# ScalarE issues the stores of gates and activations in a PEER layer, and the dense part's loads of both

## The chip, the cores and the metric

The kernel runs on one core of a Trainium2 chip. The metric is the device time of one execution, in microseconds (us). The names of the engines are those of the profile: PE (TensorE, matmuls), PEld (its weight loads), DVE (VectorE), ACT (ScalarE), POOL (GpSimd), SP (SyncE). Every engine works off its own instructions in order. A DMA is issued by one engine's queue as one of its instructions, and moves its bytes without that engine.

## What is computed

One layer of an encoder for 512 prompt tokens (four tiles of 128) and 128 tokens of eight sample streams (one more tile). The part at issue is the feed-forward half, PEER: each token picks, by a query and two sets of 128 sub-keys, 16 experts in each of 8 heads, out of 128 x 128 experts.

```
y = h + peer(rmsnorm(h))                      # h: 2048 wide
peer: q = x @ w_query; scores per head against two sets of 128 sub-keys
      the 16 best of 128 x 128 sums per head -> expert ids, softmax gates
      a = gelu(x . U[id]);  out = sum over heads and picks of  gate * a * V[id]
```

After the layer comes a last norm. Arithmetic is f32.

## The kernel before

**Matmuls.** `gemm` (L193) streams a weight matrix in blocks `raw` of two k-rows (128x2x512 f32, 512 KB, L198, a ring of four buffers, issued by SP). `split` (L141) makes of each 128x512 half a rounded copy `whi` on ACT (L143) and the rest `wlo` on DVE (L144), in rings of five (six in the last part); PE does three 128x512 matmuls for each token tile (L211, L212, L213). After each block `pump()` advances the first generator in the list `side`, in which work that goes beside the gemms is cut into steps by `yield`; `tick()` advances the list `bg`, the PEER of two token tiles by gathered rows (POOL issues the gathers, DVE does L740 and L745). The order of each engine's instructions is fixed when the program is built: a scheduler places them by the order of the program text, these rates, priorities and cost estimates of its own.

**The PEER of the other three token tiles is dense.** Three pieces matter here:

- `weights` (L775): for each of the three tiles the gates are written out as a dense matrix of 128 tokens by 16384 experts, in 32 groups of four tokens, 96 in all. A group makes one-hot vectors on DVE (L789, L795) and, for two of the four tokens, on ACT (L792, L793); four f32 matmuls on PE (L796); a copy out of PSUM on ACT (L798, tile `s`); and a store of 256 KB to DRAM (L799, tensor `wd`).
- `U(s)` (inside `dense_peer`, L802): a gemm with 512 columns of U for three tiles; ACT takes the gelu (L829, tile `S`). For s under LEAD = 12 the result is stored to DRAM (L831, tensor `ad`), because the gates don't exist yet. These twelve gemms run beside the weights stage, which is in `side`.
- `h_step(s, i, a)` (L809): loads the tile's 512 gates from `wd` (L812, through `load`, L97, whose DMA is L99), multiplies with the activation (L814, DVE), transposes the product in four 128x128 pieces (L818, PE) and splits it into HT (L820, by L143 and L144; the tiles `m`), the stationary side of the V gemms. `late(s)` (L836) does this for the stored activations of the three tiles, and loads each of them first. `late(0)` and `late(1)` come into `side` at s = 8, behind what is left of the weights.

**The switch.** After U(11), `drain()` runs what is left in `side`, one set of pools is closed and another opened (L866 to L868), with 12 `s` buffers, D_STAGE `S` buffers, D_LOAD `b` buffers, 4 `raw`, 6 `whi` and `wlo`. Then come the gemms `V(b, nb)` (L841), b = 0 to 15, with the late h_steps of b + 1 and the U gemms from 12 on between them. For b = 0 the evict of V loads the residual `x1d` (L845) and adds it (L847).

All DMAs named here are issued by SP before the change, so gates, activations, residual and weight blocks stand in one queue, in the scheduler's order.

## Time and profile before

| | |
|---|---|
| median of 3 runs | 3991.54 us (3985.18 to 3993.43) |
| the profiled execution | 3996.57 us, its span 3994.9 us |
| PE, PEld | 97%, 80% of the span |
| DVE, ACT, POOL | 79%, 43%, 21% |
| DMA | 1180.51 MB, 296 GB/s on the mean |
| granted TensorE clock, mean | 0.99 |

Stages, from the trace: the G2 tiles' query ends at about 1660 us; routing goes to 1805; the weights stage runs from 1805 to 2160, beside the U gemms; the last UT matmul before the switch starts at 2205.59, the first V matmul at 2212.34; the dense gemms then go on to the end. "Busy" counts an instruction's whole duration; matmuls overlap, so that one of some 395 ns is followed by the next after some 227 ns. Idle time of PE is what can be won or lost; on another engine it matters only where PE ends up waiting for it.

### The profile page before, as it was taken

How to read it: one execution, taken by the hardware profiler on the slowest of the kernel's cores; microseconds unless marked ns; L12 is line 12 of the kernel's file. 1: busy time of each engine (PE TensorE's matmuls, PEld its weight loads, DVE VectorE, ACT ScalarE, POOL GpSimd, SP SyncE). 2: the span in 40 equal slices, each digit the busy share in tenths (PEclk: the TensorE clock that was granted, in tenths of full speed). 3: DMA queues.
4: the chain of work that ended last, by engine and by line, in shares of the span. 5: the costliest groups of instructions: out<-in, count | busy, mean ns of one | idle time of the engine just before them, and what ended most of it. 6: DMA issues, size and time to landing. Idle time of an engine off the chain costs nothing. (4 is left out here: it accounts for less than half of the span.)

```text
span 3994.9 us, 52665 instructions
## 1 busy us (share of the span) xinstructions
PE 3883.8 (97%) x17880; PEld 3177.5 (80%) x17880; DVE 3153.5 (79%) x5421; ACT 1728.2 (43%) x3338; POOL 829.1 (21%) x678
## 2 busy tenths in 40 slices
PE   8999998999999999999999899999999999999998
PEld 6778786877777888877878788877888888888886
DVE  4655769966767987899977688878888888888888
ACT  5665554444444334436665333333333333333333
POOL 1000113211212223211111112222222222222222
PEclk9999999999999999999999999999999999999999
DMA  7666786777878997569988989989998999999987
GB/s 224 204 187 208 248 264 201 273 276 279 311 277 286 336 334 249 206 198 314 327 264 288 338 325 338 342 299 365 338 350 336 353 331 345 345 340 349 346 337 290
DMA packets 333919, 1180.51 MB, mean 296 GB/s; under 512 B 35840, under 2 KB 94784, under 8 KB 267088
## 3 DMA queue, kind: packets, MB, share of 16 engines
q1 hardware_dynamic: 259824, 640.15, 47.9%
q0 software_dynamic: 73824, 536.99, 35.0%
q8 instruction: 141, 2.31, 0.2%
q14 instruction: 130, 1.06, 0.1%
HBM read 1117.69 MB, written 59.31 MB: 295 GB/s over the span
## 5 line engine op out<-in xcount | busy, mean ns | idle before, releaser
L211 PE MATMUL acc<-whi,m 128*128 128x512 f32 (+1 forms) x5232 | 2066.7, 395 | 23.3 <-ACT whi L143 18.3
L212 PE MATMUL acc<-wlo,m 128*128 128x512 f32 (+1 forms) x5232 | 2049.8, 392 | 22.5 <-DVE wlo L144 22.4
L213 PE MATMUL acc<-whi,m 128*128 128x512 f32 (+1 forms) x5232 | 2044.1, 391 | 0.3 <-DVE m L144 0.2
L143 ACT CAST whi<-raw 128x512 fp32r<-128x512 f32 (+1 forms) x1888 | 1157.9, 617 | 1979.3 <-PE acc L213 1646.6
L144 DVE TENSOR_TENSOR wlo<-raw,whi 128x512 fp32r<-128x512 f32 (+1 forms) x1824 | 1221.5, 689 | 526.8 <-ACT whi L143 523.1
L212 PEld LDWEIGHTS acc<-wlo,m 128*128 128x128 f32 x5232 | 990.7, 189 | 227.1 <-DVE wlo L144 34.5
L211 PEld LDWEIGHTS acc<-whi,m 128*128 128x128 f32 x5232 | 989.3, 189 | 225.4 <-ACT whi L143 20.6
L213 PEld LDWEIGHTS acc<-whi,m 128*128 128x128 f32 x5232 | 989.5, 189 | 202.7 <-DVE m L144 0.8
L740 DVE SCALAR_TENSOR_TENSOR gb<-gb,xa 128x2048 f32<-128x2048 f32 x256 | 589.6, 2303 | 79.5 <-DMA gb<-in_U,idx 69.1
L745 DVE SCALAR_TENSOR_TENSOR xa<-gb,hw,xa 128x2048 f32<-128x2048 f32 x239 | 560.3, 2344 | 70.4 <-DMA gb<-in_V,idx 64.1
L754 POOL DMA_INDIRECT gb<-in_V,idx x239 | 318.5, 1333 | 1228.8 <-DVE wlo L144 331.2
L754 POOL DMA_INDIRECT gb<-in_U,idx x256 | 339.6, 1327 | 1018.9 <-ACT whi L143 366.2
L144 POOL TENSOR_TENSOR wlo<-raw,whi 128x512 fp32r<-128x512 f32 x64 | 91.5, 1431 | 261.8 <-ACT whi L143 229.7
L796 PEld LDWEIGHTS pm<-s 128*128 128x128 f32 x768 | 102.6, 193 | 30.5 <-ACT s L793 14.6
L796 PE MATMUL pm<-s 128*128 128x128 f32 x768 | 113.7, 283 | 10.0 <-DVE s L789 8.0
L789 DVE TENSOR_SCALAR s<-io,S 128x128 f32<-128x128 f32 x384 | 114.8, 339 | 3.6 <-DMA wd<-s 3.6
L847 DVE TENSOR_TENSOR s<-s,acc 128x512 f32<-128x512 f32 x180 | 112.5, 678 | 0.0
L144 DVE TENSOR_TENSOR m<-pm,m 128x512 fp32r<-128x512 f32 (+1 forms) x142 | 93.5, 661 | 7.5 <-ACT m L143 6.5
L143 ACT CAST m<-pm 128x512 fp32r<-128x512 f32 (+1 forms) x142 | 79.6, 563 | 16.3 <-PE pm L362 6.3
L798 ACT COPY s<-pm 128x512 f32<-128x512 f32 x96 | 56.5, 588 | 64.8 <-PE pm L796 64.2
L814 DVE TENSOR_TENSOR b<-b,b 128x512 f32<-128x512 f32 x36 | 24.8, 688 | 56.0 <-DMA b<-wd 53.5
L792 ACT ACTIVATE s<-io,S 128x128 f32<-128x128 f32 x192 | 66.7, 398 | 3.6 <-DVE S L782 2.3
(194 smaller groups left out, 1668.7 us busy)
## 6 DMA issues: line engine op xcount, KB each, us to landing
raw<-in_UT SPq DMA_DIRECT2D x256, 512.0 KB, 6.2
raw<-in_VP SPq DMA_DIRECT2D x256, 512.0 KB, 6.5
raw<-in_w_in SPq DMA_DIRECT2D x224, 512.0 KB, 4.6
raw<-in_w_out SPq DMA_DIRECT2D x64, 512.0 KB, 5.4
raw<-in_w_q SPq DMA_DIRECT2D x64, 512.0 KB, 4.5
wd<-s SPq DMA_DIRECT2D x96, 256.0 KB, 6.0
b<-wd SPq DMA_DIRECT2D x96, 256.0 KB, 5.2
raw<-in_w_pa SPq DMA_DIRECT2D x32, 512.0 KB, 4.2
```

Of the source, the lines that this page charges most:

```text
L143: mark[0] = nc.scalar.copy(hi, src).ins
L144: (E or nc.vector).tensor_sub(lo, src, hi.bitcast(F32))
L211: nc.tensor.matmul(o, xh, hi, start=(k == 0), stop=False)
L212: nc.tensor.matmul(o, xh, lo, start=False, stop=False)
L213: nc.tensor.matmul(o, xl, hi, start=False, stop=(k == K - 1))
L740: q = nc.vector.scalar_tensor_tensor(t, t, 1.0, xg, op0=ALU.mult, op1=ALU.mult, accum_out=dots[:, j:j + 1])
L745: q = nc.vector.scalar_tensor_tensor(y, t, hw[:, j:j + 1], y, op0=ALU.mult, op1=ALU.add)
L754: d = nc.gpsimd.indirect_dma_start(out=t, out_offset=None, in_=src, in_offset=bass.IndirectOffsetOnAxis(ap=idx[j // 32][:, j % 32:j % 32 + ...
L789: nc.vector.tensor_scalar(a, io128, tr[:, 0, t:t + 1], tr[:, 2, t:t + 1], op0=ALU.is_equal, op1=ALU.mult)
L792: nc.scalar.activation(b, io128, AF.Abs, bias=tr[:, 3, t:t + 1])
L796: nc.tensor.matmul(pw[:, t - t0, :], a, b, start=True, stop=True)
L847: nc.vector.tensor_add(y[i, nb], x1, ps)
```

## The change

The stores of gates (L799) and activations (L831) and the loads of both in the dense part are issued by ACT's queue and no longer by SP's: 96 + 36 stores and 96 + 36 loads, 264 DMAs. Weight blocks and everything else stay with SP. `load` takes a tag, and after the switch the loads of activations have a ring "h" of their own with three buffers (D_ACT); D_LOAD goes from 4 to 3 and D_STAGE from 5 to 3. `h_step` is cut differently: loads, a `yield`, the mul, a `yield`, then the transposes. `late(s)` starts the loads of tile i + 1 next to the mul of tile i. For b = 0, V loads the residual straight into the `y` slots ahead of its gemm (SP), and the add is in place. Lines move by one from L98 on and by up to 15 further down.

```diff
-D_STAGE = 5
-D_LOAD = 4
+D_STAGE = 3
+D_LOAD = 3
+D_ACT = 3
...
-        def load(src, shape=(128, 512)):
-            t = pools["wk"].tile(list(shape), F32, name=nm("b"), tag="b", bufs=cfg["b"])
-            nc.sync.dma_start(t, src)
+        def load(src, shape=(128, 512), tag="b", E=None):
+            t = pools["wk"].tile(list(shape), F32, name=nm(tag), tag=tag, bufs=cfg["b"] if tag == "b" else D_ACT)
+            (E or nc.sync).dma_start(t, src)
             return t
...
                 nc.scalar.copy(w, pw)
-                nc.sync.dma_start(wd[ti][t0:t0 + 4, :].rearrange("t (i j) -> i t j", i=128), w)
+                nc.scalar.dma_start(wd[ti][t0:t0 + 4, :].rearrange("t (i j) -> i t j", i=128), w)
...
                 def h_step(s, i, a):
                     b, hf = divmod(s, 2)
+                    if a is None:
+                        a = load(ad[s][i], tag="h" if opened[0] else "b", E=nc.scalar)
+                    w = load(wd[G[i]][:, s * 512:s * 512 + 512], E=nc.scalar)
+                    yield
+                    nc.vector.tensor_mul(w, w, a)
+                    yield
                     if (b, i) not in HT:
                         HT[b, i] = mtile([128, 2, 8, 128], F32R)
-                    w = load(wd[G[i]][:, s * 512:s * 512 + 512])
-                    nc.vector.tensor_mul(w, w, a)
-                    yield
...
-                            nc.sync.dma_start(ad[s][i], a)
+                            nc.scalar.dma_start(ad[s][i], a)
...
                 def late(s):
+                    gens = [h_step(s, i, None) for i in range(n)]
+                    next(gens[0])
                     for i in range(n):
-                        a = load(ad[s][i])
-                        yield from h_step(s, i, a)
+                        next(gens[i])
+                        if i + 1 < n:
+                            next(gens[i + 1])
+                        yield
+                        for _ in gens[i]:
+                            yield
...
                 def V(b, nb, ticks):
                     def ev(i, ps):
-                        x1 = y.get((i, nb))
-                        if b == 0:
-                            x1 = load(x1d[i][:, nb * 512:nb * 512 + 512])
-                            y[i, nb] = slot()
-                        nc.vector.tensor_add(y[i, nb], x1, ps)
+                        nc.vector.tensor_add(y[i, nb], y[i, nb], ps)
...
+                    if b == 0:
+                        for i in range(n):
+                            y[i, nb] = slot()
+                            nc.sync.dma_start(y[i, nb], x1d[i][:, nb * 512:nb * 512 + 512])
```

The scheduler then orders the engines anew. Up to about 1715 us all of them keep their order. Three places change.

PE, the end of the last UT gemm, U(11). Before, the last of the six late transposes (four L818, `pm_20605`) stand here, with 54 matmuls of that gemm still behind them and, further down, the V gemms:

```order
9005 L212 MATMUL acc_20419<-wlo_20593,m_12743 128x512
9006 L213 MATMUL acc_20419<-whi_20592,m_12744 128x512
9007 L818 MATMUL pm_20605<-ident,b_20571 128x128 [waits PE_49]
9008 L818 MATMUL pm_20605<-ident,b_20571 128x128 x3
9009 L211 MATMUL acc_20417<-whi_20614,m_12739 128x512 [waits Activation_49]
9010 L212 MATMUL acc_20417<-wlo_20615,m_12739 128x512 [waits DVE_49]
9011 L213 MATMUL acc_20417<-whi_20614,m_12740 128x512
9012 L211 MATMUL acc_20418<-whi_20614,m_12741 128x512
9013 L212 MATMUL acc_20418<-wlo_20615,m_12741 128x512
9014 L213 MATMUL acc_20418<-whi_20614,m_12742 128x512
```

After, these are the last rows ahead of the first V matmul (`acc_20725`), and the last UT matmul is row 9032:

```order
9042 L822 MATMUL pm_20448<-ident,b_20365 128x128 [waits DVE_49,Activation_49]
9043 L822 MATMUL pm_20448<-ident,b_20365 128x128 x3
9044 L822 MATMUL pm_20495<-ident,b_20457 128x128 [waits DVE_49,PE_49]
9045 L822 MATMUL pm_20495<-ident,b_20457 128x128 x3
9046 L822 MATMUL pm_20535<-ident,b_20462 128x128 [waits DVE_49,PE_49]
9047 L822 MATMUL pm_20535<-ident,b_20462 128x128 x3
9048 L822 MATMUL pm_20605<-ident,b_20533 128x128 [waits DVE_49,PE_49]
9049 L822 MATMUL pm_20605<-ident,b_20533 128x128 x3
9050 L822 MATMUL pm_20797<-ident,b_20758 128x128 [waits DVE_49,PE_49]
9051 L212 MATMUL acc_20725<-whi_20730,m_20323 128x512 [waits Activation_49]
```

All six groups of late transposes, the first one of the next h_step (`b_20758`, of b = 1), and the last seven matmuls of the weights stage now stand between the last UT matmul and the first V matmul. Before, the last weights matmul stood 198 matmuls ahead of the end of U(11). In the stage itself, the 384 L796 rows stood in 132 places between UT matmuls and now stand in 195, over 1260 UT matmuls where there were 1062.

ACT, one group of the weights stage (`s_19685` is its pair of one-hots, `s_19653` the copy of the group before it). Before:

```order
1964 L798 COPY s_19653<-pm_19636 128x512 [waits DMAHW3_49,PE_49]
1965 L792 ACTIVATE s_19685<-io_82,S_19051 128x128 [waits DVE_49]
1966 L792 ACTIVATE s_19685<-io_82,S_19051 128x128
1967 L793 ACTIVATE s_19685<-s_19685 128x128 [waits Activation_49] x2
1968 L143 CAST whi_19793<-raw_19778 128x512 [waits PE_49]
1969 L143 CAST whi_19848<-raw_19846 128x512 [waits DMAHW4_49,DVE_49,PE_49]
```

After:

```order
2188 L799 COPY s_19653<-pm_19636 128x512 [waits PE_49]
2189 L793 ACTIVATE s_19685<-io_82,S_19051 128x128 [waits DMAHW1_49]
2190 L800 DMA wd_19046<-s_19653 128x4x128 [waits Activation_49]
2191 L794 ACTIVATE s_19685<-s_19685 128x128 [waits Activation_49]
2192 L793 ACTIVATE s_19685<-io_82,S_19051 128x128
2193 L144 CAST whi_20385<-raw_20370 128x512 [waits DVE_49,PE_49]
2194 L794 ACTIVATE s_19685<-s_19685 128x128 [waits Activation_49]
2195 L799 COPY s_19701<-pm_19684 128x512 [waits PE_49]
```

The store is now a row of ACT's, between the one-hot rows of the next group, and the wait for a free buffer (DMAHW) has gone from the copy to a one-hot row. Of the 96 store rows 45 wait for a DMA.

ACT at the switch, where SP had the loads before (rows 9 below):

```order
2315 L800 DMA wd_19046<-s_20283 128x4x128 [waits Activation_49]
2316 L144 CAST m_20398<-pm_20399 128x512 [waits PE_49]
2317 L100 DMA b_20365<-wd_19046 128x512 [waits DMAHW5_49,DMAHW4_49,DMAHW7_49,DMAHW3_49,DMAHW2_49]
2318 L100 DMA b_20455<-ad_15234 128x512
2319 L100 DMA b_20457<-wd_16498 128x512
2320 L100 DMA b_20460<-ad_15235 128x512 [waits DMAHW6_49,DVE_49]
2321 L144 CAST m_20447<-pm_20448 128x512 [waits PE_49]
2322 L100 DMA b_20462<-wd_17766 128x512
2323 L100 DMA b_20531<-ad_15236 128x512 [waits DMAHW4_49,DMAHW0_49,DVE_49]
2324 L144 CAST m_20323<-pm_20495 128x512 [waits PE_49]
2325 L100 DMA b_20533<-wd_19046 128x512 [waits DMAHW1_49]
2326 L144 CAST m_20398<-pm_20535 128x512 [waits PE_49]
```

Row 2317 is the first load of gates of the third tile (`wd_19046`). It waits for five DMA semaphores, those of that tile's stores, the last of which is row 2315; the loads behind it wait in ACT's order, some also for muls (DVE) or for casts standing ahead of them. Rows 2328 and 2329 are the loads of `h_20756` and `b_20758`, whose product is transposed in PE's row 9050, and row 2334 is the first `whi` of the V gemms.

## Rows read from the trace of the kernel before

**Rows 1.** The page, its first part: busy time, share of the span and instructions of each engine.
```profile
PE 3883.8 (97%) x17880; PEld 3177.5 (80%) x17880; DVE 3153.5 (79%) x5421; ACT 1728.2 (43%) x3338; POOL 829.1 (21%) x678
```

**Rows 2.** Busy time of each engine in stretches of the program (us of the stretch, its length, then busy time and number of instructions of each engine, the granted TensorE clock, the DMA engines' share and GB/s). In order: the weights stage, the switch, the first V gemms, and the bulk of the dense stage.
```profile
1810.00:2160.00 350.00, 340.04 (x1831) 284.47 (x1831) 305.20 (x730) 230.24 (x613) 50.10 (x41) 0.99 0.92 303
2160.00:2215.00 55.00, 48.63 (x221) 39.51 (x220) 35.28 (x38) 19.12 (x32) 9.55 (x8) 0.96 0.83 292
2215.00:2300.00 85.00, 80.39 (x357) 65.98 (x356) 63.54 (x75) 27.47 (x47) 15.30 (x11) 0.97 0.93 346
...
2750.00:3750.00 1000.00, 998.15 (x4482) 824.93 (x4481) 847.40 (x971) 346.94 (x568) 265.40 (x196) 1.00 0.92 344
```

**Rows 3.** What TensorE waited for between 1805 and 2310 us (engine, tile and line, what released it: us in total, times, longest).
```profile
PE pm L796 <- DVE s L789: 8.0, 1, 8.0
PE acc L211 <- ACT whi L143: 6.4, 1, 6.4
...
PE pm L818 <- DVE b L814: 4.6, 2, 3.3
PE pm L796 <- ACT s L793: 1.0, 1, 1.0
```

**Rows 4.** The timeline of SyncE's queue around the longest wait of rows 3 (start, us, what was issued).
```profile
2043.18 0.33 SPq L99 DMA_DIRECT2D b<-wd  x1
```

**Rows 5.** The timeline of VectorE in the same stretch (in brackets the idle time before, and what ended it).
```profile
2049.20 0.69 DVE L814 TENSOR_TENSOR b<-b,b 128x512 f32<-128x512 f32 x1 [8.68 <-DMA b<-wd]
```

**Rows 6.** Two short stretches with the columns of rows 2: right after that wait, and right after the switch.
```profile
2050.00:2060.00 10.00, 9.11 (x37) 7.84 (x38) 8.30 (x22) 4.28 (x12) 0.00 (x0) 0.67 0.43 115
...
2212.00:2220.00 8.00, 7.66 (x23) 5.87 (x24) 7.68 (x10) 4.23 (x8) 4.11 (x2) 0.68 1.04 417
```

**Rows 7.** The timeline of TensorE at the switch: the last matmul of the last UT gemm and the first three of the first V gemm.
```profile
2205.59 0.39 PE L213 MATMUL acc<-whi,m 128*128 128x512 f32 x1
2212.34 0.80 PE L211 MATMUL acc<-whi,m 128*128 128x512 f32 x1 [6.37 <-ACT whi L143]
...
2213.66 0.63 PE L213 MATMUL acc<-whi,m 128*128 128x512 f32 x1
2214.09 0.63 PE L211 MATMUL acc<-whi,m 128*128 128x512 f32 x1
```

**Rows 8.** The timeline of ScalarE at the switch.
```profile
2204.66 2.05 ACT L829 ACTIVATE S<-acc,stats 128x512 f32<-128x512 f32 x3 [8.22 <-PE acc L213]
2211.67 1.14 ACT L143 CAST whi<-raw 128x512 fp32r<-128x512 f32 x2 [4.97 <-DMA raw<-in_VP]
```

**Rows 9.** The timeline of SyncE's queue at the switch.
```profile
2205.38 1.68 SPq L831 DMA_DIRECT2D ad<-S  x3
2207.22 0.34 SPq L198 DMA_DIRECT2D raw<-in_VP  x1
```

**Rows 10.** ScalarE's groups of instructions in the weights stage, 1810 to 2160 us (line, tiles, shapes, count, busy us, mean ns of one, idle us before them and what ended it).
```profile
L143 ACT CAST whi<-raw 128x512 fp32r<-128x512 f32 x118 | 72.3, 617 | 50.5 <-PE acc L213 50.2
L792 ACT ACTIVATE s<-io,S 128x128 f32<-128x128 f32 x188 | 65.3, 398 | 3.3 <-DVE S L782 2.0 <-DMA wd<-s 1.3
L798 ACT COPY s<-pm 128x512 f32<-128x512 f32 x95 | 55.9, 588 | 64.4 <-PE pm L796 63.8 <-DMA wd<-s 0.3
L793 ACT ACTIVATE s<-s 128x128 f32<-128x128 f32 x189 | 47.1, 298 | 0.0
L829 ACT ACTIVATE S<-acc,stats 128x512 f32<-128x512 f32 x21 | 13.4, 683 | 0.4 <-PE acc L213 0.4
```

**Rows 11.** The transfers that write or read `wd`, 1805 to 2160 us (duration of the issuing instruction in ns, min/median/max; last, the time from issue to landing).
```profile
L799 SPq DMA_DIRECT2D wd<-s x96: 359/360/1568, 1809.1 to 2158.8; - x96
...
DMA to landing us min/median/max: 2.3/6.0/12.5
```

**Rows 12.** DMA issues between 2155 and 2163 us (count, KB each, median us to landing).
```profile
wd<-s SPq DMA_DIRECT2D x2, 256.0 KB, 3.4
b<-wd SPq DMA_DIRECT2D x1, 256.0 KB, 3.7
```

**Rows 13.** What SyncE's queue waited for between 1700 and 2520 us.
```profile
SPq L799 <- ACT s L792: 150.4, 82, 5.1
SPq L99 <- DVE b L814: 70.3, 31, 5.8
SPq L831 <- ACT S L829: 54.6, 29, 20.2
```

**Rows 14.** The page, its fifth part (columns as in rows 10): a gather step of VectorE, the weights stage's matmuls, and the cast and the mul of one h_step.
```profile
L745 DVE SCALAR_TENSOR_TENSOR xa<-gb,hw,xa 128x2048 f32<-128x2048 f32 x239 | 560.3, 2344 | 70.4 <-DMA gb<-in_V,idx 64.1
...
L796 PE MATMUL pm<-s 128*128 128x128 f32 x768 | 113.7, 283 | 10.0 <-DVE s L789 8.0
...
L143 ACT CAST m<-pm 128x512 fp32r<-128x512 f32 (+1 forms) x142 | 79.6, 563 | 16.3 <-PE pm L362 6.3
...
L814 DVE TENSOR_TENSOR b<-b,b 128x512 f32<-128x512 f32 x36 | 24.8, 688 | 56.0 <-DMA b<-wd 53.5
```

**Rows 15.** The chain of work that ended last, 2180 to 2320 us (start, us, what): the transposes of one h_step and the matmuls after them.
```profile
2296.12 1.09 PE pm L818 x4
2297.20 0.43 PE acc L211
...
2299.73 0.23 PE acc L212
```

More of the change, by code (lines that the diff above doesn't have):

```diff
@@ L857, in dense_peer @@
                 gf = {}
+                opened = [False]
                 steps[0] = SW
@@ L868, in dense_peer @@
                 open_work("d")
+                opened[0] = True
                 steps[0] = 1.0
```

## The prediction

> **What bounds the kernel now.** The page says first that PE is busy for 97% of the span [rows 1]: only its idle time, and the time it runs at the lower clock, can be won. The busy time by stretches shows where that time lies: 10 us idle in the weights stage, 6.4 at the switch, 4.6 in the first V gemms, and 2 in the thousand us after 2750 [rows 2]. The waits of PE name four of them by what ended them [rows 3], and the timelines show what stood behind each.
>
> - Stall 1, at 2043. PE waits 8.0 us for a one-hot of DVE [rows 3]. DVE itself stood at a mul of an h_step for 8.68 us [rows 5], because the gates it multiplies were asked for only at 2043.18 [rows 4].
> - Stall 2, the switch. The last UT matmul starts at 2205.59, the first V matmul at 2212.34 [rows 7]. ACT could not cast because the first block of VP had not landed [rows 8], and SP issued that block only after three stores of activations [rows 9].
> - Stall 3, two waits of transposes for muls, 4.6 us in sum [rows 3], late loads again.
>
> After each of them PE runs at 1.2 GHz for a while: matmuls start 0.43 us apart [rows 7, 15] where 0.23 is the pace at full speed [rows 15], and the granted clock of the 10 us after stall 1 and of the 8 us after stall 2 is 0.67 and 0.68 [rows 6]. From these, 8 us x 0.64 at half speed are 5.1 us, which cost 2.6; so stall 2 costs 6.5 + 2.6 = 9.1 us. Stall 1 likewise costs 8.0 + 2.3 = 10.3, stall 3 some 4.6 + 1.0 = 5.6.
>
> **Term 1, stall 1: -10.3.** In the new order no mul of a late h_step stands inside the weights stage on DVE; all come at its end. What DVE would wait for is no longer there. The ends are -10.3 and 0 (if another load holds DVE, the nearest row being this one); I take -10.3.
>
> **Term 2, the switch: +18.** Before, the six late transposes were spread among UT matmuls. Now all of them, the first of b = 1, and seven weights matmuls stand between the last UT matmul and the first V matmul, and the loads that feed them stand on ACT behind the last store of gates. So what was hidden by UT matmuls becomes a chain, counted from the end of the last UT matmul:
>
> - ACT has two gelus (0.68 each), two copies (0.59), two activations of 0.40, two of 0.30, a cast (0.56) and five issues (0.33 to 0.36) to the end of the last store's issue [rows 8, 10, 11, 14]: 6.0 us.
> - The first load of the third tile's gates waits for that store to land, then must land itself. Landings of these 256 KB transfers took 2.3 us at the least and 6.0 at the median in the busy weights stage [rows 11], 3.4 and 3.7 around 2155 [rows 12]. The chain stops the weight stream when its ring of four blocks is full, so I take 4.5: 9.0 for the two.
> - Mul 0.69 and cast 0.56 [rows 14], transposes 0.5 (half of the 1.09 for four at the low clock [rows 15]): 1.75. Behind them a load in a reused buffer, 4.5, then mul, transposes and cast up to ACT's next issue, 1.9.
> - Two issues, 0.7, and the loads of `h_20756` and `b_20758`, 4.5, then a mul, 0.7. Two gather steps of DVE of 2.34 [rows 14] stand among these muls and lie beside the landings. The residual's loads and the first VP block stand on SP, and land in this time too.
>
> That is 6.0 + 9.0 + 1.75 + 4.5 + 1.9 + 0.7 + 4.5 + 0.7 = 29.0 us to the first V matmul. Of it PE works some 4.9 on what it did elsewhere before: 25 transposes (3.4) and seven two-pass matmuls of 0.28 a pass at most (under 4, overlapped some 1.5) [rows 14, 15]. So 24.1 idle, plus 2.6 for the lower clock behind it, minus the old 9.1: +17.6, rounded to 18. With all four landings at 2.3 it is +9, at 6.0 +24; these ends are kept. The value is nearer to the middle because two landings fall where nothing but gathers is moving. The smaller rings, D_STAGE and D_LOAD 3, act within this chain: a load that needs a used buffer waits for its mul, and that is counted.
>
> **Term 3, stall 3: -4.5.** Its loads are issued one step ahead now, and those of the first h_step of b = 1 even stand in the chain of term 2. Ends -5.6 and 0 (the mul waits 70.3 us of SP's time for a free buffer [rows 13], and three `b` buffers free no earlier than four).
>
> **Term 4, the weights stage: +1.** ACT takes on 96 stores at 0.36 us [rows 11], 34.6 us, and 36 stores of activations at about 0.33. Before, ACT stood idle for 50.5 + 64.4 us in this stage, waiting for PE [rows 10]: that hides them as long as ACT does not come late. Per group of four tokens, PE needs some 4.1 us (1260 UT matmuls at 0.227 and 113 us of weights matmuls [rows 14], by 96), and ACT 0.59 + 2 x 0.40 + 2 x 0.30 + 1.5 casts of 0.62 + gelu and issues 0.6 = 3.5 us [rows 10, 11], issues included; 0.6 us a group are left for waits. The upper end is that the issues show in full, +34.6; the lower that they show nowhere and the stage's small waits go too, -1.6 (what rows 3 have beside stall 1 in this stage, 1.0, and pieces under that). I take +1, near the lower end, because ACT's work fits into PE's with the issues in it; the 1 is for the 63 additional places at which PE goes from one kind of matmul to the other.
>
> **Term 5, the rest: 0.** From 2750 on PE loses 2 us in 1000 [rows 2]; loads and muls of later h_steps stand some forty rows ahead on ACT, so there is nothing to gain and, by that distance, nothing lost. The 36 loads and the moved residual take 0.3 us of issue each on engines that have idle time. SP loses 264 issues; it waited 150.4 us at stores of gates for ACT [rows 13], which held the weight blocks behind them, but those came in time except at the switch.
>
> Sum: -10.3 + 18 - 4.5 + 1 = **+4 us**. The profiled run took 3996.6, 5.0 above the median 3991.5, so it gives about 4000.8 on the profile's own base and **3996** on that of the runs. A difference below 0.2% (8 us) can't be told from none.
>
> **A rule weighed.** The rows at the stores show where SP's time goes: waits for ACT of 150.4 us at 82 of them [rows 13], against 0.36 us of issue each [rows 11]. The Trainium skill, "DMA: Bandwidth & Descriptors", section "Issuing engines are not separate DMA queues", says that DMAs started by the scalar, sync or gpsimd engine run on the same 16 DMA engines, and that starting them on several saves only the sequencer's issue time, usually small. By that rule the move of 264 issues would be worth their issue time at most and the time would stay 3991.5, which is case D; the trace agrees on the size of an issue, and has beside it waits that an in-order queue takes along.
>
> **Rivals.**
>
> - **B, slower: ACT falls behind in the weights stage.** 45 of the 96 stores, and the loads, wait for an earlier DMA's semaphore in ACT's order, and behind a waiting store stand the one-hots and casts PE needs. It decides where that wait exceeds the 0.6 us cover a group on average; landings of 6.0 at the median and 12.5 at most [rows 11] make that possible. 0.2 us beyond, 96 times, is +19: with the rest, 3991.5 + 4 - 1 + 19 = 4014. For it: rows 11's spread. Against it: at 4.1 us a group most stores have landed two groups later.
> - **C, faster: the chain at its quickest.** Landings of 2.3 make the switch +9, both other stalls vanish whole, and so do the small waits: 9 - 10.3 - 5.6 - 1.6 = -8.5, or 3983. Against it: five transfers in a row would all have to be the fastest seen.
> - **D, nothing: the issuing queue does not matter.** Transfers land at the pace of the DMA engines whoever asks, and the late loads' waits only move from stalls 1 and 3 to the switch: with landings of 3.7 there [rows 12] its term is 17.6 - 4 x 0.8 = 14.4, against 10.3 + 4.5 = 14.8 taken away, and without term 4 the sum is 0: 3991.5.
>
> **How the numbers follow.** Forecast A (+4) 0.53 (its own range 3990 to 4002); B 0.22; C 0.12; D 0.13. The range leaves out a tenth at each side: below it a C with more luck than its sum, above it B with the switch at +24 or a weights stage nearer to +34.6. So 3983 to 4015. Under -8 us lies most of C only: 0.10. Above +8 us lie B and the part of A whose landings take 5.5 us and more (4 x 1.0 on top of +4), some 0.10 of the 0.53: together 0.32. The rest is within 0.2%: 0.58.
>
> **What would show it.** Right: no wait of 8 us on PE in the weights stage; a gap of some 25 to 30 us between the last UT and the first V matmul in which PE does only transposes and a few weights matmuls; ACT's first load of gates there idle for the last store; the stretch from 2750 on unchanged in length. Wrong: a switch as short as before, or PE waiting for ACT's one-hots or casts by more than a few us in the weights stage, or new waits in the dense stage.

## The result and the profile after

The change takes 4041.5 us (median of 4, 4036.79 to 4043.59) against 3991.55: ratio 1.0126, 95% interval 1.0111 to 1.0140, so 50 us slower where +4 was forecast. The profiled execution took 4043.59 us, span 4041.9, 47.0 more than the span before.

The stretches of [rows 2], in the kernel after:

```profile
1810.00:2160.00 350.00, 339.40 (x1794) 286.81 (x1793) 292.49 (x668) 225.94 (x566) 51.24 (x41) 0.99 0.90 298
2160.00:2215.00 55.00, 43.56 (x241) 37.01 (x239) 30.32 (x83) 30.28 (x76) 3.87 (x2) 0.95 0.51 154
2215.00:2300.00 85.00, 59.18 (x245) 46.69 (x246) 57.87 (x64) 20.84 (x37) 13.42 (x12) 0.79 0.93 338
2750.00:3750.00 1000.00, 991.93 (x4447) 817.79 (x4446) 839.46 (x973) 343.59 (x564) 256.81 (x195) 1.00 0.92 343
```

The weights stage is about as before (339.40 us busy of 350, where it was 340.04). The loss begins at the switch: 11.4 us idle, then 25.8 idle with the granted clock at 0.79, and 8 us in the thousand after 2750 where there were 2. The waits of PE that answer to [rows 3]:

```profile
PE pm L822 <- DVE b L816: 27.8, 5, 13.4
PE acc L213 <- DVE wlo L145: 13.0, 6, 4.8
PE pm L797 <- DVE s L790: 8.3, 4, 6.1
PE pm L797 <- ACT s L794: 2.7, 2, 1.4
```

27.8 us of waits for muls of late h_steps, all at the switch; wlo 13.0, the first of them the routing's 4.8, which [rows 3] leaves out and the change does not touch; and at L797 still a wait of 6.1. That last one is stall 1 in a new place. DVE, 2094 us, answering to [rows 5]:

```profile
2094.83 0.69 DVE L816 TENSOR_TENSOR b<-b,b 128x512 f32<-128x512 f32 x1 [7.75 <-DMA b<-wd]
```

A late mul again stands among the one-hots and waits 7.75 us for its gates, and PE's 6.1 us are the wait for the one-hot behind it.

**The switch.** The last UT matmul starts at 2200.25, the first V matmul at 2238.00: 37.7 us, the "gap" in what follows.

```profile
2200.25 0.40 PE L214 MATMUL acc<-whi,m 128*128 128x512 f32 x1
...
2238.00 1.20 PE L212 MATMUL acc<-whi,m 128*128 128x512 f32 x2
```

ACT's timeline (answering to [rows 8]; ACTq are the DMAs it issues):

```profile
2205.38 0.38 ACTq L800 DMA_DIRECT2D wd<-s  x1
2205.80 0.58 ACT L144 CAST m<-pm 128x512 fp32r<-128x512 f32 x1 [0.45 <-PE pm L822]
2212.17 0.37 ACTq L100 DMA_DIRECT2D b<-wd  x1
...
2213.05 0.45 ACTq L100 DMA_DIRECT2D b<-wd  x1
2219.02 0.35 ACTq L100 DMA_DIRECT2D b<-ad  x1
...
2221.71 0.33 ACTq L100 DMA_DIRECT2D b<-wd  x1
...
2231.96 0.33 ACTq L100 DMA_DIRECT2D h<-ad  x1
2232.33 0.69 ACTq L100 DMA_DIRECT2D b<-wd  x1
...
2235.31 1.14 ACT L144 CAST whi<-raw 128x512 fp32r<-128x512 f32 x2 [2.76 <-DMA h<-ad]
```

DVE's muls in the same stretch:

```profile
2218.30 0.69 DVE L816 TENSOR_TENSOR b<-b,b 128x512 f32<-128x512 f32 x1 [8.04 <-DMA b<-wd]
2219.74 0.69 DVE L816 TENSOR_TENSOR b<-b,b 128x512 f32<-128x512 f32 x1 [0.75 <-DMA b<-wd]
...
2224.35 0.68 DVE L816 TENSOR_TENSOR b<-b,b 128x512 f32<-128x512 f32 x1
2229.99 0.69 DVE L816 TENSOR_TENSOR b<-b,b 128x512 f32<-128x512 f32 x1 [4.96 <-DMA b<-wd]
...
2237.06 0.69 DVE L816 TENSOR_TENSOR b<-b,h 128x512 f32<-128x512 f32 x1 [0.65 <-DMA b<-wd]
```

The chain of the prediction is there, link by link: last store of gates issued at 2205.38, the first load of its tensor only at 2212.17 (the store has landed, 6.4 us after its issue ended); mul at 2218.30; a load in a reused buffer at 2221.71, its mul at 2229.99; cast, loads at 2231.96 and 2232.33, mul at 2237.06. Beside it SP has waits of its own, which the prediction did not price. SP's waits in 2200 to 2245 us, and its timeline (answering to [rows 9]):

```profile
SPq L864 <- DMA wd<-s: 41.5, 1, 41.5
SPq L864 <- DMA b<-ad: 10.2, 2, 6.4
SPq L199 <- DVE b L816: 7.1, 1, 7.1
```

```profile
2212.29 11.28 SPq L864 DMA_DIRECT2D s<-x1d  x3
2230.75 7.47 SPq L199 DMA_DIRECT2D raw<-in_VP  x4
```

The residual's load into a new `y` slot (L864) waits 41.5 us, till that same store, which reads an `s` tile, has landed; by that releaser the slot lies in memory that the old `s` tiles held. Two more such loads follow, till 2223.57. The wait for the store is not the last one. Behind it V's first block waits 7.1 us more, for a mul (L199 <- DVE b), and goes out at 2230.75, just after the mul of 2229.99 ends. The likely reason is that the block's new buffer lies where a late `b` tile lay; that is read from the releaser and not tested by itself. V's first block thus hangs on the chain of the late h_steps. Before, it was issued at 2207.22 [rows 9].

**The dense stage.** One of its stalls, at 2437 to 2451 us; first ACT, then DVE:

```profile
2437.72 0.62 ACT L144 CAST whi<-raw 128x512 fp32r<-128x512 f32 x1 [1.22 <-PE acc L214]
2448.28 0.33 ACTq L100 DMA_DIRECT2D h<-ad  x1
2448.72 0.62 ACT L144 CAST whi<-raw 128x512 fp32r<-128x512 f32 x1 [10.38 <-PE acc L214]
```

```profile
2447.55 0.69 DVE L816 TENSOR_TENSOR b<-b,h 128x512 f32<-128x512 f32 x1 [6.21 <-DMA b<-wd]
2448.16 0.68 DVE L145 TENSOR_TENSOR wlo<-raw,whi 128x512 fp32r<-128x512 f32 x1
```

DVE waits 6.21 us for gates; ACT's next load needs the buffer that this mul frees, so it is issued only at 2448.28, and the cast behind it in ACT's order, which needed none of this, waits 10.38 us (the page puts that to PE, which had long been done with the buffer's last matmul). The six `whi` in stock cover most of it, not all: PE waits 0.38 us for the `wlo` of 2448.16. In the whole dense stage casts waited 67.9 us behind such muls:

```profile
ACT whi L144 <- DVE b L816: 67.9, 15, 9.5
```

### The profile page after: what moved, and what is told of

Read it like the earlier page. It is cut to its first block, busy times and chain, and to the rows that moved or that the text cites. A ratio compares the mean times of both kernels' runs of the same rounds, so it can differ in the third digit from the quotient of the medians.

```text
span 4041.9 us, 52484 instructions
## 1 busy us (share of the span) xinstructions
PE 3893.9 (96%) x17880; PEld 3184.9 (79%) x17880; DVE 3152.3 (78%) x5421; ACT 1732.6 (43%) x3338; POOL 811.4 (20%) x678
## 2 busy tenths in 40 slices
DMA packets 333917, 1180.50 MB, mean 292 GB/s; under 512 B 35840, under 2 KB 94784, under 8 KB 267088
## 3 DMA queue, kind: packets, MB, share of 16 engines
q0 software_dynamic: 73824, 536.99, 34.8%
## 4 chain that ended last, share of the span: by engine, by line
PE 68%; DMA 14%; DVE 10%; issue 6%; ACT 1%; SPq 0%; POOL 0%; ACTq 0%; DVEq 0%; POOLq 0%
PE acc L213 21%; PE acc L214 21%; PE acc L212 21%; DMA gb<-in_U,idx 6%; DVE wlo L145 3%; PE pm L797 2%; DMA b<-wd 2%; DVE xa L746 1%; DMA gb<-in_V,idx 1%; DVE gb L741 1%; DMA wd<-s 1%; PE pm L306 1%; PE pm L822 1%; DVE s L854 1%; PE pm L287 1%
## 5 line engine op out<-in xcount | busy, mean ns | idle before, releaser
L212 PE MATMUL acc<-whi,m 128*128 128x512 f32 (+1 forms) x5232 | 2068.3, 396 | 17.6 <-ACT whi L144 12.2
L755 POOL DMA_INDIRECT gb<-in_V,idx x239 | 309.7, 1296 | 1274.6 <-DVE wlo L145 420.4
L755 POOL DMA_INDIRECT gb<-in_U,idx x256 | 328.3, 1282 | 1043.1 <-ACT whi L144 342.2
L797 PEld LDWEIGHTS pm<-s 128*128 128x128 f32 x768 | 115.9, 193 | 31.8 <-ACT s L794 9.4
L797 PE MATMUL pm<-s 128*128 128x128 f32 x768 | 120.6, 279 | 11.2 <-DVE s L790 8.3
L799 ACT COPY s<-pm 128x512 f32<-128x512 f32 x96 | 56.4, 588 | 97.5 <-PE pm L797 95.9
L822 PE MATMUL pm<-ident,b 128*128 128x128 f32 x384 | 60.4, 281 | 28.6 <-DVE b L816 27.8
L822 PEld LDWEIGHTS pm<-ident,b 128*128 128x128 f32 x384 | 49.1, 144 | 42.4 <-issue 29.2
```

Source lines behind the costliest of these rows:

```text
L212: nc.tensor.matmul(o, xh, hi, start=(k == 0), stop=False)
L755: d = nc.gpsimd.indirect_dma_start(out=t, out_offset=None, in_=src, in_offset=bass.IndirectOffsetOnAxis(ap=idx[j // 32][:, j % 32:j % 32 + ...
L797: nc.tensor.matmul(pw[:, t - t0, :], a, b, start=True, stop=True)
L822: nc.tensor.transpose(pt[:, j, :], w[:, j * 128:j * 128 + 128], ident)
```

## The experiments

Ratios are to the kernel before on the same chip. "Gap" is from the start of the last UT matmul to that of the first V matmul. For the other columns the 15,696 gemm matmuls of a trace are numbered in their order on PE, and the time between two numbers is compared with the trace before: no. 6,951 to 8,208 (the weights stage, to the end of U(11)), 8,209 to 8,709 (the first V gemms), 8,709 to the last. They are of one profile each, and e1, whose time is that of before, shows that such columns differ by some 8 us from chance and from waits that only change places. The profiles of e2 and e7 are those of their fastest runs, with spans 0.2 us below and 2.5 us above that of before, so their columns hold little of what the medians lose.

| run | median us | ratio, 95% | gap | to U(11) | first V | rest |
|---|---|---|---|---|---|---|
| before | 3991.55 | | 6.8 | | | |
| the change | 4041.50 | 1.0126 (1.0111 to 1.0140) | 37.7 | -6.6 | +7.0 | +14.8 |
| e1 all on SP | 3991.87 | 1.0006 (0.9996 to 1.0016) | 10.2 | -5.4 | -6.5 | +7.9 |
| e2 stores on SP | 4003.72 | 1.0043 (1.0026 to 1.0060) | 12.8 | -4.2 | -6.6 | +5.5 |
| e18 the same | 4004.02 | 1.0035 (1.0025 to 1.0046) | 13.7 | -4.0 | -5.6 | +10.2 |
| e3 loads on SP | 4021.28 | 1.0077 (1.0060 to 1.0094) | 33.8 | -7.4 | +2.5 | +7.0 |
| e7 gate stores only | 4004.19 | 1.0044 (1.0031 to 1.0058) | 18.8 | -15.8 | +7.7 | -0.1 |
| e14 activation stores only | 3988.82 | 1.0002 (0.9991 to 1.0014) | 3.1 | -8.5 | -1.3 | -3.4 |
| e4 rate 2.2 | 4077.15 | 1.0215 (1.0198 to 1.0232) | 19.6 | +49.4 | -7.0 | +18.1 |
| e6 rate 2.0 | 4051.78 | 1.0142 (1.0110 to 1.0175) | 25.8 | +22.2 | +2.0 | +17.3 |
| e8 residual late | 4039.19 | 1.0124 (1.0105 to 1.0143) | 34.8 | -6.4 | +14.2 | +12.6 |
| e13 both | 4052.62 | 1.0175 (1.0155 to 1.0194) | 11.1 | +19.8 | +20.6 | +6.0 |
| e5 same gates | 4024.49 | 1.0083 (1.0060 to 1.0107) | 38.6 | -16.2 | -0.3 | +12.2 |
| e17 dense loads on SP | 4023.56 | 1.0087 (1.0065 to 1.0109) | 35.6 | -9.8 | -0.1 | +7.0 |
| e16 only dense loads on ACT | 3998.49 | 1.0027 (1.0012 to 1.0041) | 13.6 | -9.7 | -6.6 | +18.9 |
| e9 e6, loads tied | 4098.46 | 1.0274 (1.0243 to 1.0304) | 24.2 | +21.2 | +4.7 | +59.4 |
| e10 change, loads tied | 4073.66 | 1.0234 (1.0205 to 1.0263) | 36.7 | -7.8 | +1.8 | +47.1 |
| e11 e2, loads tied | 4051.57 | 1.0169 (1.0147 to 1.0192) | 9.6 | -2.7 | -6.4 | +47.5 |
| e12 e2, rings of four | 4009.32 | 1.0063 (1.0040 to 1.0085) | 7.9 | -5.5 | +4.4 | +7.0 |
| e15 e2, five whi | 4013.04 | 1.0064 (1.0050 to 1.0079) | 13.5 | -4.0 | -4.4 | +9.4 |

### Which of the moves costs

**e1**, from the kernel after (as all but e7 and e14):

```diff
-                nc.scalar.dma_start(wd[ti]...
+                nc.sync.dma_start(wd[ti]...
-                            nc.scalar.dma_start(ad[s][i], a)
+                            nc.sync.dma_start(ad[s][i], a)
-                    ... E=nc.scalar)          # both loads of h_step
+                    ... )
```

> The change with all its DMAs back on SP (new rings, loads one step ahead and the residual into y stay). Theory 1, ACT's queue is the cause (stores on ACT reorder the end of the LEAD gemms, loads on ACT hold casts): about the time of before, 3985 to 4000 us. Rival 2, the smaller rings and the residual's early loads are the cause, whichever queue issues: 4015 us or more, with the losses after 2250 us still there.

3991.87, ratio 1.0006. Theory 1 holds and rival 2 falls: rings, loads one step ahead and the residual cost nothing that these runs could tell while SP issues.

**e2** and **e18** put the two store lines alone back on SP.

> Stores of gates and activations back on SP, loads on ACT as in the change. Theory 1: the late transposes are again ahead of the last UT matmul, so the gap at the switch is 15 us or less where the change has 37.7, and stall 1 of before may come back; ACT's casts still wait for loads in the dense stage (some +15 to 20 us after the switch): 4005 to 4018 us. Rival 2: no change from 4041 in the dense stage, the same range. Rival 3, that only the stores' issue slots on ACT count: 3991 us.

> Stores on SP, loads on ACT once more, for a second profile: the first fell on the fastest of its four runs (3996 of 3996 to 4009) and shows little loss. Theory 7: in a run near 4004 us the loss lies after the switch, as waits of PE for wlo, each behind an ACT cast that stood behind a load; 3996 to 4010 us.

+17 us, and +14 the second time, by the ratios. **e3** puts the two loads alone back.

> Loads of gates and activations back on SP, stores on ACT as in the change. Theory 1: the gap at the switch stays above 25 us, since the order at the end of the LEAD gemms hangs on the stores; the dense stage loses at most 5 us against before, and casts wait for no mul there: 4015 to 4028 us. Rival 2: the dense stage loses 15 us as in the change, 4035 to 4045 us.

+31 us, with the gap at 33.8. So loads on ACT cost some 14 to 17, stores on ACT some 31; together 45 to 48 of the 50: the two parts add up, as closely as the intervals (4 to 7 us to a side) allow.

**e7** changes one line of the kernel before: `nc.sync.dma_start(wd[ti]...` becomes `nc.scalar.dma_start(wd[ti]...`.

> The kernel before, with nothing changed but the 96 stores of gates, issued by ACT. Theory 1: this alone reorders the end of the LEAD gemms (20 of the 24 late transposes after or within 26 matmuls of the last UT matmul), and costs most of what the stores cost in the change: 4005 to 4022 us. Rival 3, the issue slots on ACT are what costs (0.36 us each, 35 us): the same sum, but then the loss grows evenly over the weights stage and not at the switch. If the residual's early load has a part in it: 3990 to 4005 us.

+17 us. The profile, of the fastest of its eight runs, shows only 2.5 of them. It has a longer switch and longer first V gemms (gap +12.1, then +7.7) and a weights stage that is 15.8 shorter, in part by work that moved behind it. So a loss that grows evenly over the weights stage is not there, and 96 issues of 0.36 us on ACT show no cost by themselves; that the new order makes the whole 17 is likely, not shown. The other 14 us that e3 has over e7 come only with the rest of the change. The traces put them in the gap (33.8 against 18.8). In e7 the last store of gates is issued 6.2 us ahead of the last UT matmul, in e3 3.5 us and in the change 5.1 us behind it; where SP issues the stores (e1, e2, e16, e18) it is 46.8 us ahead, and the gap is 10.2 to 13.7. In all three with gate stores on ACT V's first block goes out just after a late mul. The residual is not what holds e3: its first loads are out by 2219.7, and V's block still waits for a mul, till 2226.68. Which part of the change moves the last store so far back was not tested.

**e14** does the same with the activations' stores alone (`ad[s][i]`).

> The kernel before, with only the 36 stores of activations issued by ACT; the order of the other engines stays nearly as it was. Before, SP stood 20.2 us at these three stores for the gelu, with V's first block behind them. If that wait sets stall 2 (6.75 us from the last UT to the first V matmul, and the lower clock after it), the block is now loaded ahead and the gap falls below 3 us: 3980 to 3985 us, ratio 0.9975 to 0.9990. If the block also waits for the new pools' memory: no change, 3986 to 3991 us.

No difference, 1.0002. Its profile has a gap of 3.1 and a span of 3976.4, but it is the fastest of 12 runs (3978.13 to 3998.24): a shorter gap that the median does not show. No version here beats the kernel before.

### What holds the switch

**e4** sets `SW = 2.2`, **e6** `SW = 2.0` (1.6 in the change).

> The change, with the steps of the side work per weight block in the LEAD gemms raised from 1.6 to 2.2 (SW), so that the weights stage ends some 310 UT matmuls before the switch and its six late transposes stand among UT matmuls. Theory 1: the gap at the switch falls below 15 us, which gives back some 20 to 28 us; the dense stage's losses stay: 4010 to 4022 us, more if the denser weights stage makes PE wait for one-hots. Rival 3, that the weights stage's issue slots on ACT cost the time: no gain, 4040 us or more.

> The change with 2.0 steps of side work per weight block in the LEAD gemms in place of 1.6: the last weights matmul stands 168 UT matmuls ahead of the switch, and all six late transposes among UT matmuls. Theory 1: the gap at the switch is below 16 us, and of the change's loss some 15 us come back, less what PE waits for one-hots where weights groups follow each other without UT matmuls (2.2 steps lost 27 us in such waits, here one run of six groups is left, so under 12): 4020 to 4038 us. If the gap stays above 25 us theory 1 has the wrong place.

Both miss: slower than the change. The transposes are ahead of the switch, and what they gave is lost two to three times over in the weights stage, where the scheduler now sets groups side by side with no UT matmul between. PE's waits in e4 from 1805 us on:

```profile
PE pm L797 <- ACT s L794: 26.9, 22, 1.4
```

Sixteen such groups in a row wait 1.43 us each for ACT's one-hot between 1991 and 2047 us, a group taking 3.71 us, with the granted clock at 0.50 from 2000 to 2050. And the gap is still 19.6 and 25.8. In e6 the late muls are done, and SP stands at the residual's loads till a store of activations has landed. First SP's waits (2195 to 2265 us), then its timeline, then ACT's:

```profile
SPq L864 <- DMA ad<-S: 30.4, 2, 29.8
```

```profile
2244.61 11.74 SPq L199 DMA_DIRECT2D raw<-in_VP  x4
```

```profile
2260.28 0.62 ACT L144 CAST whi<-raw 128x512 fp32r<-128x512 f32 x1 [23.71 <-DMA raw<-in_VP]
```

V's first block goes out 9.5 us after the last UT matmul (2235.15), and 15.7 us more pass till ACT can cast it, with the loads of b = 1 beside it. So SP's barrier is only part of this gap.

**e8** undoes the residual: the load moves from in front of V's gemm back to its evict, into a `b` buffer.

```diff
-                        nc.vector.tensor_add(y[i, nb], y[i, nb], ps)
+                        x1 = y.get((i, nb))
+                        if b == 0:
+                            x1 = load(x1d[i][:, nb * 512:nb * 512 + 512])
+                            y[i, nb] = slot()
+                        nc.vector.tensor_add(y[i, nb], x1, ps)
...
-                    if b == 0:
-                        for i in range(n):
-                            y[i, nb] = slot()
-                            nc.sync.dma_start(y[i, nb], x1d[i][:, nb * 512:nb * 512 + 512])
```

> The change with the residual loaded at the evict of V again, by SP, into a b buffer. In the change SP waited 41.5 us at the first of the early residual loads for the last store of gates, with V's weight blocks queued behind. If that wait sets the gap, it falls from 37.7 to 25 us or less and the time to 4025 us; if the chain of late h_steps sets it, as theory 1 has it, only the first transpose of b = 1 leaves the chain: 29 to 34 us, 4033 to 4039 us.

34.8, as for the chain, and no time won (4039.19): the first V gemms lose what the gap gives. SP (2195 to 2245 us) is not free either; V's first block now stands at the head of its queue and waits for late loads and then for the last late mul (2228.43 to 2229.12):

```profile
SPq L199 <- DMA b<-ad: 52.0, 1, 52.0
...
SPq L199 <- DVE b L816: 5.1, 1, 5.1
```

```profile
2229.19 22.62 SPq L199 DMA_DIRECT2D raw<-in_VP  x8
```

It lands after 6.5 us, and the first V matmul waits for its cast. The same holds in e3 and e17, where V's first block goes out 28.1 and 30.0 us after the last UT matmul, again just after a late mul. So in the change the residual's loads are not what holds V's blocks; the late h_steps are. **e13** joins e6 and e8.

> The change with 2.0 steps per weight block (late transposes ahead of the switch) and the residual loaded at the evict again: both together. Theory 6, two barriers of about the same length at the switch: the chain of late h_steps (alone taken away by the 2.0 steps: gap 25.8) and SP's residual loads, which stand ahead of V's blocks and wait for the last stores to land (alone taken away: gap 34.8). With both gone the gap is 14 us or less, and the time 4030 to 4042 us against 4052 with the rate alone. If a third cause holds the gap: still above 20 us, 4046 us or more.

The gap falls to 11.1, so there were two barriers, the late h_steps (34.8 in e8) and the early residual (25.8 in e6, the landing of the block included), and taking away either alone leaves the other. But the time stays at 4052.62: the first V gemms take 20.6 us longer. The expectation is right on the gap and wrong on the time. The loads that were moved are waited for elsewhere: between 2224 and 2390 us DVE waits 14.7 us for the residual at V's evict, and casts wait 30.8 us behind those adds and 26.9 behind late muls. What each of these costs PE is not shown.

**e5** reads the late h_steps' gates ahead of the switch from `wd[G[0]]`.

> The change, but the six late h_steps ahead of the switch read their gates from the first of the three tiles' tensors (so their products are not the reference's): their loads then need not wait for the last store of the third tile. Theory 1, a chain that begins at the last store: the gap between the last UT and the first V matmul falls from 37.7 to between 22 and 30 us, and the time to 4026 to 4036 us. Rival, the gap is set by the new pools' memory becoming free or by landings alone: still 35 us or more, 4038 to 4045 us.

The rival is right on the gap (38.6). The time fell as theory 1 had it, but through the stage before (-16.2 against the change's -6.6) and the first V gemms (-0.3 against +7.0). So a gap of this length does not need the late loads' wait for the last store of gates, the chain's first link. The chain formed anew behind the loads of b = 1: six of them issued between 2218.73 and 2221.7, the gates landing after 14.4 us at the median, beside V's four blocks:

```profile
raw<-in_VP SPq DMA_DIRECT2D x4, 512.0 KB, 6.7
...
b<-wd ACTq DMA_DIRECT2D x3, 256.0 KB, 14.4
```

### The loads on ACT

**e16** (stores and late loads on SP, loads after the switch on ACT) and **e17** (the reverse for the loads, stores on ACT):

```diff
-                    ... E=nc.scalar)                                     # both loads
+                    ... E=nc.scalar if opened[0] else nc.sync)           # e16
+                    ... E=nc.sync if opened[0] else nc.scalar)           # e17
```

> Of the change's moves to ACT only the loads after the switch; the stores and the late loads ahead of the switch stay on SP. Theory 7: in the dense stage a load that waits on ACT for a mul holds the casts behind it, and this is the whole price of loads on ACT (17 us where all loads were on ACT): 4000 to 4010 us. If the price belongs to the late loads ahead of the switch: 3986 to 3994 us.

> The change with only the loads after the switch back on SP; stores and the late loads ahead of the switch stay on ACT. Theory 7: the dense stage's loss goes, as with all loads on SP: 4018 to 4026 us against 4041, with no cast waiting for a mul after the switch. If the late loads on ACT are what the 20 us between these two kernels are: 4036 us or more.

18 us come back in e17, 20 in e3, the same within their intervals; e16 pays 11 (interval 5 to 16; expected 12 to 22). So the price of loads on ACT is paid after the switch. The casts' waits behind muls after 2245 us, in e16 and in e17:

```profile
ACT whi L144 <- DVE b L816: 65.5, 12, 11.8
```

```profile
ACT whi L144 <- DVE b L816: 12.7, 6, 5.0
```

**e9**, **e10** and **e11** tie each load on ACT behind the cast that precedes it in the program, and put the h_steps of b = 1 behind the first V gemm, in e6, the change and e2.

```diff
-            (E or nc.sync).dma_start(t, src)
+            q = (E or nc.sync).dma_start(t, src)
+            if E is not None and opened_d[0]:
+                after(q.ins)
...
-                    if b < LEAD // 2 - 1:
-                        side.append(late(2 * b + 2))
-                        side.append(late(2 * b + 3))
                     for nb in range(4):
+                        if nb == (b == 0) and b < LEAD // 2 - 1:
+                            side.append(late(2 * b + 2))
+                            side.append(late(2 * b + 3))
```

> The kernel of 2.0 steps (late transposes already ahead of the switch, yet a gap of 25.8 us there), with the late h_steps of b = 1 put in behind the first V gemm and their loads tied behind the cast before them in the program, so that ACT can't issue six loads ahead of V's first casts. Theory 4, a burst: with V's first blocks and the residual, 4.3 MB are asked for within 12 us, and the DMA engines (400 GB/s there) give V's first block after 15 us: gap 14 us or less, 4030 to 4042 us against 4052. Rival, V waits for the new pools' memory, whatever is loaded beside: gap still above 20 us, 4046 us or more.

> The change with the same edit: loads of b = 1 behind the first V gemm and not ahead of V's casts. The six late h_steps of b = 0 stay a chain behind the last store. Theory 1 with 4: the chain to the last of the six transposes stays, 25 to 31 us of gap in place of 37.7, and the first V gemms lose less to late casts: 4022 to 4035 us against 4041. If the loss after the switch is not from these loads: 4036 us or more.

> Stores on SP, loads on ACT, with the same edit. With the stores on SP the change lost 17 us (4003.7). Theory 4: the loss is ACT's loads going out ahead of the casts, in a burst at the switch and held for muls in front of casts later; with each load behind its cast 3984 to 3996 us, about the time of before or of all on SP. If casts are still held behind loads that wait for a buffer: 3998 to 4006 us.

All three miss, by 39 to 56 us, and theory 4 falls. In e9 there is no burst ahead of V's first casts and the gap is the same: SP stood at the residual's loads for 35.8 us, for a store of activations. And the dense stage, where only the loads' place and their tie to a cast changed, loses 32 to 42 us against the same kernel without the edit (e6, the change, e2). With loads one step ahead and not some forty rows, DVE waits for gates (e11, after 2245 us) three times as long as the 39.3 before:

```profile
DVE b L820 <- DMA b<-wd: 124.3, 41, 6.9
```

Casts wait longer for V's blocks there too (167.1 us in e11, 66.5 in e2); which of the two waits costs PE was not split.

**e12** sets `D_LOAD = 4`, `D_ACT = 4`, `D_W = 5` in e2; **e15** sets `D_W = 5` alone.

> Stores on SP, loads on ACT, rings of four buffers for gates and for activations in place of three (the room comes from whi and wlo, five in place of six). Theory 5: a load whose buffer is not free waits in ACT's queue for a mul and holds the casts behind it (71 us of such waits in the profile with stores on SP); a fourth buffer takes most of these waits away: under 30 us of them, and 3988 to 3998 us in place of 4003.7. If ring waits are not what costs: 4000 to 4010 us, more if five whi are too few.

> Stores on SP, loads on ACT, rings of three as in the change, but five whi and wlo in place of six: the control for the run with rings of four, which gave up the sixth for them. If the fourth buffers helped and the lost sixth whi hid it: 4013 to 4025 us, slower than that run's 4009. If neither matters: 4000 to 4012 us.

Casts wait 47.8 us behind muls in e12, fewer than e2's 71.1 but not under 30:

```profile
ACT whi L144 <- DVE b L816: 47.8, 11, 11.0
```

Against before, the ratios are 1.0063 for e12 and 1.0064 for e15, with intervals of 9 and 6 us to a side: no gain from the fourth buffers is seen. So that ring waits are the price is not shown; that the issuing queue is, by e3, e16 and e17. Nor is it shown that the casts' waits behind muls make up the price: e2's profile has 71.1 us of them in a span as long as that of before.

## Why the prediction was wrong

- **Term 1 (-10.3): wrong in fact.** "No mul of a late h_step stands inside the weights stage on DVE" holds for four of the six. The first two (1961 and 2094 us) still stand ahead of the last one-hots, and one of them stopped DVE for 7.75 us and PE for 6.1. The stretch to U(11) became 6.6 us shorter, of which 4.9 is work moved behind it by the prediction's own estimate; the forecast made it 14.2. Error 8. (Stall 1 was also priced by a slip: of the 10 us after it [rows 6] 6.6 ran at half speed, 0.9 of them idle, which costs 2.9 and not 2.3.)
- **Term 2 (+18): the chain right, its landings too short, and a link missing.** The gap was 37.7, forecast 29.0. Engine work came out at 12.2 us where 11 was put in (the first link's parts add up to 6.2, not 6.0); the four transfers took 6.4, 6.1, 8.3 and 4.7, together 25.5, where 18.0 was put in. The bound of 6.0 each, kept for the range, was the better value. The missing link is V's first block: that it and the residual's loads "land in this time too" passed over what they wait for. The block went out only after a late mul, 30.5 us after the last UT matmul; in e3, e8 and e17 its landing is what the first V matmul waits for. Error 9.
- **Term 3 (-4.5): wrong.** The first V gemms lost 7.0. Stall 3 went, but casts stood behind loads on ACT (30.1 us behind muls between 2239 and 2375 us) and the weight blocks came late (24.7 us of casts' waits there, 9.4 before). How much each costs is open: e7, with its loads on SP, lost 7.7 here. Error 11.5.
- **Term 4 (+1): right.** PE waits 2.7 us for ACT's one-hots from the weights stage to the switch, and e7's profile shows no loss there. Rival B put ACT's in-order waits in the wrong stage: casts held behind a waiting DMA are seen in the dense stage.
- **Term 5 (0): wrong.** +14.8 in the profile, and loads on ACT after the switch cost 11 to 18 by e2, e16, e17 and e18. "Some forty rows ahead" is a distance in the order; a load that waits for its buffer uses that distance up, and on ACT the casts behind it wait too. On SP it was weight blocks that stood behind such a wait, with four blocks in stock.
- **Rival D falls.** Its time, 3991.5, is what e1 gives, where SP issues everything; that the issuing queue does not matter is refuted by e2 and e3. The Trainium skill, "DMA: Bandwidth & Descriptors", section "Issuing engines are not separate DMA queues", says that DMAs started by the scalar, sync or gpsimd engine run on the same 16 DMA engines, and that starting them on several saves only the time to issue them. The bytes are the same here (1180.50 MB against 1180.51), but the time did not stay as it was: the order and the waits that came with the new queue cost 50 us, and the measurement decides.

The steps that failed are thus the landings and the missing link of term 2, the nothing of term 5, and what terms 1 and 3 counted as won. Left open: which part of the change moves the last store of gates behind the last UT matmul (the 14 us between e7 and e3), and which of the dense stage's waits make up the loads' price.

## What to carry over

Moving a DMA to another queue moves its wait, so list what stands behind it there: on ACT it was the casts that feed every matmul, with some 12 us in stock (an estimate: six `whi`, each good for nine matmuls 0.227 us apart). A chain of loads whose data was just stored is priced at the median landing or above (6.0 us in the weights stage [rows 11], 6.4 on the mean in this chain), since the transfers that follow a stall are issued together. Where a pool is closed and another opened, look up which old tile lies under each of the first new loads, weight blocks too, and when its last store lands or its last reader is done.

## Not expected

Spreading the same loads later, one step ahead of their use, cost 32 to 42 us in the dense stage (e9 to e11), as much as or more than the longer gap of the change (31 us). A rate of side work raised from 1.6 to 2.2 put weights groups next to each other, and PE at 1.2 GHz (granted clock 0.50) for 50 us (e4).
